# Feed-forward block: the output projection as seven block products of eight, presums started at the input's split, GpSimd left with masks and accumulating DMAs

## The chip, the cores and the metric

One NeuronCore of one Trainium2 chip runs the kernel. The metric is device time in microseconds (us) of one execution; lower is better. Engines are called as the profile calls them: PE (TensorE matmul), PEld (its weight load), DVE (VectorE), ACT (ScalarE), POOL (GpSimd), SP (SyncE, which here only issues DMAs; SPq and POOLq are the queues).

## The reference

One layer of a hybrid encoder over 528 positions (16 learned ones and 512 frames), width 1024, float32:

```python
u  = rmsnorm(h, norm_mix_w)
proj = u @ w_in                         # 1024 x 8208, cut into c, q, k, v, z, a, b, gates
y_conf = silu(layernorm(conv31(c_val * sigmoid(c_gate)))) @ w_conf_out
y_dn = (rmsnorm(gated_delta_rule(silu(conv4(q, k, v)), a, b)) * silu(z)) @ w_dn_out
g_conf, g_dn = split(sigmoid(gate_logits + b_gate))
h = h + (g_conf * y_conf + g_dn * y_dn) @ w_out
u2 = rmsnorm(h, norm_ffn_w)
up = conv3(u2 @ w_up)                   # 1024 x 5632
h = h + (silu(up_gate) * up_val) @ w_down
out = rmsnorm(h, norm_final_w)[:, 16:]
```

## The kernel before

All activations lie transposed, 128 channels on the partitions and the positions along the row, so that a product is a sum over eight channel tiles with the weights as the stationary operand. Every float32 product is made of three passes of a rounded format: the high parts of both factors, high by low, and low by high. `weights` loads one 128x1024 tile of weights into a buffer `wr` (three of them) by a DMA on SP, has ACT cast it to the high part `wh` and DVE subtract to the low part `wl` (two buffers each). `gemm` then issues 8 x 3 x 2 = 48 matmuls of some 260 columns for one output tile of 128 channels.

The stages, with the names of their tiles: keys (`k`) and small decay terms; the convolution branch (`cg`, `cv`, with 30 taps a channel tile on DVE into `ca`); eight heads of the delta rule (`q`, `v`, then short chains `kS`, `wP`, `S`, `o`, whose matmuls are interleaved with products `ga`, `z`); `layer_norm`; the two branch projections (`y`, 8 + 8 tiles, scaled by the gates in `gt`); the output projection (`wo`, 8 tiles); the feed-forward's first product (`up`, 6 tiles, then 19 pairs in `sx` and `sz`); its second product (`dn`); the final norm.

The 19 pairs are made by `seven`: a 256x256 block product in halves, as seven products of 128-row blocks and not eight, each of 12 matmuls of 258 columns (4 pairs of channel tiles x 3 passes), 84 for a pair of output tiles where `gemm` issues 96. Seven products need sums of weight blocks and sums of input blocks. `factors` makes the latter on DVE, one call for two channel tiles, and splits them with ACT and DVE. The former are made ahead by `presums`, all in HBM (tiles `ws`): two plain copies (each 512 KB), then an accumulating DMA of 512 KB and two of 256 KB, each waiting for the one before. In the kernel before all five are on POOL's queue, start after the last mask (`masks[-1]`), and two sets are in flight at a time: the copies of set m wait for the end of set m-2.

POOL also does the masks (`affine_select` in `decays`), 23 memsets of four columns ahead of a convolution row (`ra`, in `out_raw` and `conv4`), 4 memsets `LL` and 32 block copies into `mn` (in `grow`).

A scheduler inside the program (`Plan`) sets the order: it records the operations, gives each a modelled price, and places them by list scheduling with the due times of a table (`BIAS`, `LNP`, `IVP`, `UP`, `WP`). Each engine then runs its list strictly in that order, and so does each DMA queue: an instruction that waits holds up everything behind it on its engine. Every instruction is emitted at line 469, so the profile is read by tile names.

Of the kernel before, what the change touches and what calls it, by code (L numbers as in the profile page):

```python
# [230 lines left out]
class Plan:  # L231
# [66 lines left out]
    def price(self, eng, fn, a, k, out):  # L298
# [10 lines left out]
        if fn == "dma_start":  # L309
            if eng == "POOL":  # L310

                return 1000, int(np.prod(out.shape)) * 4 / 140.0
            return 475, int(np.prod(out.shape)) * 4 / 290.0 * (1 if self.run(k) >= P else 2)
# [158 lines left out]
def record(A, out):  # L472
# [65 lines left out]
    def presums(src, n, hold):  # L538
# [3 lines left out]
        for m in range(n):  # L542
          with plan.at(1):
# [195 lines left out]
    for k in range(KT + 1):  # L739
      with plan.at(UP):  # L740
# [106 lines left out]
    def conv4(acc, t, way=None):  # L847

        c = bt(n="cv")
        if way:  # L850
            a = acc
            if way == "copy":
                a = bt(n="ra")
                G.memset(a[:, :PAD], 0.0)
# [88 lines left out]
    masks, softs = [], []  # L943
# [46 lines left out]
    def grow(h0):  # L990
# [218 lines left out]

    wus = presums(A['wuq'], FT - NPRE, masks[-1])  # L1210
# [55 lines left out]
    mh, ml = [], []  # L1266
# [11 lines left out]
    for f in range(KT):  # L1278
        x = bt(n="xr")
        SY.dma_start(out=x[:, :TW], in_=A['xT'][f][:, T0:T])  # L1280
        acc = p2("wo")
        gemm(acc, weights(A['wo'][f]), mh, ml, MIDR)
# [223 lines left out]
```

## Time and profile before

| | |
|---|---|
| time, median of 3 runs | 1016.2 us (1014.99 to 1018.35) |
| the profiled execution's own time | 1018.73 us |
| its span, first to last instruction | 1016.9 us |
| mean granted TensorE clock | 0.994 |
| busy: PE / DVE / ACT / POOL | 98% / 75% / 52% / 11% of the span |
| DMA moved | 157.39 MB, mean 155 GB/s |

The profile page is of one execution. A busy PE is not PE at its peak: matmuls overlap, and one that waits a short while can still count as busy; how fast products run is read from the distance of matmuls in the chain of work, not from the busy share. Waits name the engine that came last.

### The profile page before, as it was taken

How to read it: one execution, taken by the hardware profiler on the slowest of the kernel's cores; microseconds unless marked ns; L12 is line 12 of the kernel's file. 1: busy time of each engine (PE TensorE's matmuls, PEld its weight loads, DVE VectorE, ACT ScalarE, POOL GpSimd, SP SyncE). 2: the span in 40 equal slices, each digit the busy share in tenths (PEclk: the TensorE clock that was granted, in tenths of full speed). 3: DMA queues.
4: the chain of work that ended last, by engine and by line, in shares of the span. 5: the costliest groups of instructions: out<-in, count | busy, mean ns of one | idle time of the engine just before them, and what ended most of it. 6: DMA issues, size and time to landing. Idle time of an engine off the chain costs nothing.

```text
span 1016.9 us, 20105 instructions
## 1 busy us (share of the span) xinstructions
PE 995.6 (98%) x8202; PEld 949.7 (93%) x8202; DVE 766.4 (75%) x1304; ACT 526.2 (52%) x945; POOL 108.4 (11%) x172
## 2 busy tenths in 40 slices
PE   9999999999999999999999999999999999999996
PEld 6999999999989998989999999999999999988886
DVE  5988959689979998989485455599998988832334
ACT  5688732263644554355373224467786766632222
POOL 0011221523421222120000000000000000000000
PEclk9999999999999999999999999999999999999998
DMA  6144698988688897883313244424555556643332
GB/s 224 63 124 97 174 208 218 254 161 191 178 152 203 217 221 158 206 195 87 123 63 110 98 167 138 133 84 145 176 179 184 189 164 185 206 136 101 99 93 83
DMA packets 67932, 157.39 MB, mean 155 GB/s; under 512 B 15104, under 2 KB 21632, under 8 KB 67840
## 3 DMA queue, kind: packets, MB, share of 16 engines
q1 hardware_dynamic: 51728, 116.26, 36.1%
q0 software_dynamic: 16112, 39.85, 20.4%
q8 instruction: 64, 1.05, 0.4%
q14 instruction: 28, 0.23, 0.1%
HBM read 150.78 MB, written 45.16 MB: 193 GB/s over the span
## 4 chain that ended last, share of the span: by engine, by line
PE 72%; DMA 12%; issue 6%; DVE 5%; ACT 3%; POOL 1%; SPq 0%; DVEq 0%; ACTq 0%; POOLq 0%
PE dn L469 12%; PE sx L469 10%; PE y L469 9%; DMA ws<-in_wuq 7%; PE sz L469 7%; PE wo L469 5%; PE cv L469 5%; PE ga L469 4%; PE cg L469 4%; PE up L469 3%; PE z L469 2%; PE v L469 2%; DMA ws<-ws 2%; DMA eg<-d_e 2%; PE q L469 2%
## 5 line engine op out<-in xcount | busy, mean ns | idle before, releaser
L469 DVE TENSOR_TENSOR wl<-wr,wh 128x1024 fp32r<-128x1024 f32 (+2 forms) x195 | 225.6, 1158 | 156.0 <-PE dn L469 61.6
L469 ACT CAST wh<-wr 128x1024 fp32r<-128x1024 f32 (+2 forms) x195 | 193.8, 996 | 222.0 <-PE dn L469 56.4
L469 DVE SCALAR_TENSOR_TENSOR ca<-c,par,ca 128x516 f32<-128x516 f32 (+10 forms) x240 | 178.4, 750 | 6.3 <-ACT ca L469 2.3
L469 DVE SCALAR_TENSOR_TENSOR uy<-up,par,uy 128x512 f32<-128x512 f32 x88 | 64.2, 746 | 1.8 <-ACT uy L469 1.4
L469 POOL DMA_DIRECT2D ws<-in_wuq x57 | 49.3, 872 | 151.3 <-DMA ws<-in_wuq 77.7
L469 PE MATMUL dn<-fh,wh 128*128 128x512 f32 (+1 forms) x171 | 61.8, 369 | 0.0
L469 PE MATMUL dn<-fl,wh 128*128 128x512 f32 (+1 forms) x171 | 61.8, 369 | 0.0
L469 PE MATMUL sx<-nh,wh 128*128 128x258 f32 x228 | 60.5, 289 | 1.2 <-ACT wh L469 0.9
L469 PE MATMUL sz<-nl,wh 128*128 128x258 f32 x228 | 59.8, 283 | 0.0
L469 PE MATMUL sx<-nl,wh 128*128 128x258 f32 x228 | 59.4, 282 | 0.0
L469 PE MATMUL sz<-nh,wh 128*128 128x258 f32 x228 | 59.4, 283 | 0.0
L469 PE MATMUL ga<-ul,wh 128*128 128x258 f32 (+1 forms) x256 | 59.0, 294 | 0.0
L469 PE MATMUL ga<-uh,wh 128*128 128x258 f32 (+1 forms) x256 | 58.7, 294 | 0.0
L469 DVE SCALAR_TENSOR_TENSOR cv<-ra,par,cv 128x528 f32<-128x528 f32 x69 | 50.8, 758 | 6.2 <-POOL ra L469 5.9
L469 PE MATMUL ga<-uh,wl 128*128 128x258 f32 (+1 forms) x256 | 48.4, 295 | 0.0
L469 POOL DMA_DIRECT2D ws<-ws x38 | 35.8, 951 | 93.6 <-DMA ws<-in_wuq 58.8
L469 PEld LDWEIGHTS sx<-nh,wh 128*128 128x128 f32 x228 | 43.1, 189 | 2.9 <-ACT wh L469 1.4
L469 PE MATMUL sz<-nh,wl 128*128 128x258 f32 x228 | 44.6, 283 | 0.0
L469 PEld LDWEIGHTS sx<-nl,wh 128*128 128x128 f32 x228 | 43.2, 190 | 0.0
L469 PEld LDWEIGHTS sz<-nh,wh 128*128 128x128 f32 x228 | 42.9, 189 | 0.1
L469 PEld LDWEIGHTS sz<-nl,wh 128*128 128x128 f32 x228 | 42.9, 189 | 0.0
L469 PEld LDWEIGHTS ga<-ul,wh 128*128 128x128 f32 x256 | 42.7, 192 | 0.3
(324 smaller groups left out, 2764.7 us busy)
## 6 DMA issues: line engine op xcount, KB each, us to landing
wr<-in_win SPq DMA_DIRECT2D x64, 512.0 KB
ws<-in_wuq POOLq DMA_DIRECT2D x57, 512.0 KB, 7.9
wr<-ws SPq DMA_DIRECT2D x38, 512.0 KB
ws<-ws POOLq DMA_DIRECT2D x38, 256.0 KB, 6.1
wr<-in_wuq SPq DMA_DIRECT2D x19, 512.0 KB
wr<-in_wd SPq DMA_DIRECT2D x17, 512.0 KB
wr<-in_wuq SPq DMA_DIRECT2D x19, 256.0 KB
wr<-in_wdn SPq DMA_DIRECT2D x8, 512.0 KB
```

The source lines that it names most:

```text
L469: getattr(engines[o.eng], o.fn)(*(get(x) for x in o.a), **{n: get(x) for n, x in o.k.items()})
```

## The change

The output projection goes through `seven` as well: 4 pairs of output tiles, 28 block products of 12 matmuls, in place of 8 `gemm` calls of 48. For that, `factors` is called for each two finished tiles of the mix (tiles `mt`, `mq`, `mh`, `ml`, `mhl`), the results are added by DVE straight into the residual (`use`), and `w_out` gets four sets of presums. All presums now start once the input is split (`done`), the 4 sets of `w_out` first. Their two plain copies go from POOL's queue to SP's. The memsets go from POOL to DVE, the copies into `mn` to ACT. The scheduler's price of an accumulating DMA and its table of due times are others, so the order of the whole program differs.

```diff
-                return 1000, int(np.prod(out.shape)) * 4 / 140.0
+                return 1000, int(np.prod(out.shape)) * 4 / 122.0
...
-            G.dma_start(out=r[m][:, 0:2], in_=src[:, m, 0:3:2])
+            SY.dma_start(out=r[m][:, 0:2], in_=src[:, m, 0:3:2])
             plan.after = set(h)
-            G.dma_start(out=r[m][:, 2:4], in_=src[:, m, 0:2])
+            SY.dma_start(out=r[m][:, 2:4], in_=src[:, m, 0:2])
             G.dma_start(out=r[m][:, 1:3], in_=src[:, m, 3:4].broadcast_to([P, 2, HD]), accum_op=ALU.add)
...
-        G.memset(a[:, :PAD], 0.0)
+        V.memset(a[:, :PAD], 0.0)
...
+    softs, done = [], max(j for _, j, w in uh[-1].tl.hist if w)
+    wos = presums(A['wo'], KT // 2, done)
+    wus = presums(A['wuq'], FT - NPRE, done)
...
-            G.memset(l[0:32, :, 32:64], 0.0)
+            V.memset(l[0:32, :, 32:64], 0.0)
...
-                G.tensor_copy(out=Mn[h][r, :, r], in_=D8(h)[r])
+                S.copy(out=Mn[h][r, :, r], in_=D8(h)[r])
...
-
-    wus = presums(A['wuq'], FT - NPRE, masks[-1])
...
-        a, b = split(y[:, :TW], TW, "m")
-        mh.append(a)
-        ml.append(b)
+        ys.append(y)
+        if f % 2:
+            with plan.at("mf"):
+                mb.append(factors(*ys[f - 1:], HW, "m"))
...
-        acc = p2("wo")
-        gemm(acc, weights(A['wo'][f]), mh, ml, MIDR)
-        V.scalar_tensor_tensor(out=halves(x[:, :TW], HW), in0=acc[:, :, MID], scalar=0.5, in1=halves(x[:, :TW], HW),
-                               op0=ALU.mult, op1=ALU.add)
...
+    for m in range(KT // 2):
...
+        x0, x1 = hs[2 * m:]
+        where = {'p1': (x0, 0, 0.5), 'c11b': (x0, 0, 0.5), 'u2': (x0, 1, 0.5), 'c12b': (x0, 1, 0.5),
+                 'u3': (x1, 1, -0.5), 'c22b': (x1, 1, -0.5), 'c21': (x1, 0, -0.5)}
+
+        def use(what, acc):
+            x, b, by = where[what]
+            xb = x[:, b * HW:(b + 1) * HW]
+            V.scalar_tensor_tensor(out=xb, in0=acc, scalar=by, in1=xb, op0=ALU.mult, op1=ALU.add)
+
+        seven(A['wo'], m, wos, mb, HW, use)
```

Of the table only this is shown, since its numbers tell a reader nothing: `SWITCH` 375 to 750, `LNP` -146 to 74, `IVP` 2165 to 665, `UP` 519 to 0, `WP` 214 to 174, and all of `BIAS`. What it does to the order stands below at three places.

**POOL's queue** in the heads stage, before. `ws` are the presums (number of the set, then a serial number), `ra` is the convolution row of a head.

```order
L469 DMA ws_9_3520<-ws_9_3520 128x512
L469 DMA ws_10_3546<-ws_10_3546 128x512
L469 DMA ws_9_3520<-ws_9_3520 128x512
L469 MEMSET ra_10_2071 128x4
L469 DMA ws_10_3546<-ws_10_3546 128x512
L469 DMA ws_11_3988<-in_wuq 128x2x512
L469 DMA ws_12_4037<-in_wuq 128x2x512
L469 DMA ws_11_3988<-in_wuq 128x1024
```

After the change the same queue holds accumulating DMAs alone there; neither memsets nor plain copies (the 128x1024 ones) are left on it:

```order
L469 DMA ws_13_3203<-in_wuq 128x2x512
L469 DMA ws_14_3274<-in_wuq 128x2x512
L469 DMA ws_13_3203<-ws_13_3203 128x512
L469 DMA ws_14_3274<-ws_14_3274 128x512
L469 DMA ws_13_3203<-ws_13_3203 128x512
L469 DMA ws_14_3274<-ws_14_3274 128x512
```

**SP's queue** in the heads stage, after the change: the plain copies stand among the loads of weights (`wr`) and of the heads' decay rows (`eg`), and from the copies of sets 15 and 16 to those of sets 17 and 18 there are two loads of weights. Before, the queue had only the loads there.

```order
L469 DMA wr_40_3634<-in_win 128x1024
L469 DMA ws_15_3660<-in_wuq 128x2x512
L469 DMA ws_16_3754<-in_wuq 128x2x512
L469 DMA ws_15_3660<-in_wuq 128x1024
L469 DMA ws_16_3754<-in_wuq 128x1024
L469 DMA eg_3_3856<-d_e_1_835 128x528
L469 DMA wr_41_3932<-in_win 128x1024
L469 DMA eg_4_3946<-d_e_1_835 128x528
L469 DMA wr_42_4009<-in_win 128x1024
L469 DMA ws_17_4120<-in_wuq 128x2x512
L469 DMA ws_18_4164<-in_wuq 128x2x512
```

**The start of the output projection**, after the change. First DVE, from the scaling of the last branch tile (`y_16`) to the first result of a block product (`sx_1`); `gt_6` and `gt_15` are the last two mix tiles, `ml_10` to `ml_12` the low parts of their factors:

```order
L469 SCALAR_TENSOR_TENSOR gt_6_5102<-gt_6_5102,y_16_7508 128x516
L469 TENSOR_TENSOR gt_6_5102<-gt_6_5102,gt_2_3909 128x516
L469 TENSOR_TENSOR gt_15_6441<-gt_6_5102,gt_15_6441 128x258
L469 SCALAR_TENSOR_TENSOR mt_4_7491<-mt_4_7491,gt_6_5102 128x258
L469 TENSOR_TENSOR ml_10_7625<-gt_6_5102,mh_10_7620 128x2x258
L469 SCALAR_TENSOR_TENSOR mq_4_7630<-mt_4_7491,gt_6_5102 128x258
L469 TENSOR_TENSOR ml_11_7634<-gt_15_6441,mh_11_7623 128x2x258
L469 TENSOR_TENSOR ml_12_7642<-mt_4_7491,mh_12_7628 128x2x258
L469 TENSOR_TENSOR mhl_4_7637<-mq_4_7630,mhl_4_7637 128x258
L469 SCALAR_TENSOR_TENSOR xr_1_7467<-sx_1_7586,xr_1_7467 128x258
```

And PE there: twelve matmuls stand between the last of `y_16` and the first row that needs a factor of the last two tiles (`mh_10`); the rows below begin with the last two of the twelve.

```order
L469 MATMUL sz_1_7595<-mh_4_7344,wh_81_7494 128x258
L469 MATMUL sz_1_7595<-ml_4_7352,wh_81_7494 128x258
L469 MATMUL sz_1_7595<-mh_10_7620,wh_81_7494 128x258
L469 MATMUL sx_1_7586<-mh_11_7623,wh_81_7494 128x258
L469 MATMUL sz_1_7595<-ml_10_7625,wh_81_7494 128x258
L469 MATMUL sz_1_7595<-mh_7_7545,wl_81_7516 128x258
L469 MATMUL sz_1_7595<-mh_1_7268,wl_81_7516 128x258
L469 MATMUL sz_1_7595<-mh_4_7344,wl_81_7516 128x258
L469 MATMUL sz_1_7595<-mh_10_7620,wl_81_7516 128x258
L469 MATMUL sx_1_7586<-ml_11_7634,wh_81_7494 128x258
```

Before, `y_16` needed one addition and one split to follow it on DVE, and the first `wo` product had its other seven channel tiles to go through.

## Rows read from the trace of the kernel before

**Rows 1.** The page: the span, and each engine's busy time.

```profile
span 1016.9 us, 20105 instructions
...
PE 995.6 (98%) x8202; PEld 949.7 (93%) x8202; DVE 766.4 (75%) x1304; ACT 526.2 (52%) x945; POOL 108.4 (11%) x172
```

**Rows 2.** Busy time by stage: from:to length, engines, PEclk, DMA share, GB/s.

```profile
180.00:470.00 290.00, 282.03 (x2664) 271.60 (x2664) 256.14 (x392) 140.72 (x289) 85.06 (x130) 0.99 0.82 189
...
603.00:650.00 47.00, 47.00 (x390) 46.92 (x389) 25.42 (x32) 17.77 (x23) 0.00 (x0) 1.00 0.52 160
650.00:882.00 232.00, 230.64 (x1896) 227.97 (x1895) 210.83 (x325) 163.46 (x262) 0.00 (x0) 1.00 0.53 165
```

**Rows 3.** The chain that ended last: start, length, what, matmul count.

```profile
602.70 46.55 PE wo L469 x384
...
736.83 2.90 PE sx L469 x24
```

**Rows 4.** Timeline, 294 to 297 us: start, length, engine, instruction, [idle before it].

```profile
295.10 0.39 POOL L469 MEMSET ra<- 128x4 f32 x1
...
295.53 0.77 DVE L469 SCALAR_TENSOR_TENSOR cv<-ra,par,cv 128x528 f32<-128x528 f32 x1 [2.83 <-POOL ra L469]
...
296.61 0.49 PE L469 MATMUL wP<-r,mn 128*128 128x128 f32 x2 [2.33 <-DVE r L469]
```

**Rows 5.** Busy time by stage, as rows 2, around that hole.

```profile
280.00:300.00 20.00, 17.64 (x134) 16.47 (x133) 15.51 (x30) 8.91 (x25) 4.91 (x7) 0.95 0.84 138
```

**Rows 6.** Groups of instructions by form: count, busy us, mean ns, idle before.

```profile
L469 POOL COPY mn<-DU 32x128 f32<-32x128 f32 x32 | 18.9, 596 | 2.8 <-DMA DU<-d_x 1.6
...
L469 ACT COPY mn<-gX 32x128 f32<-32x128 f32 x16 | 4.1, 255 | 0.2
```

**Rows 7.** Timeline of DVE, 741 to 746 us, where it works without a pause.

```profile
741.33 0.68 DVE L469 TENSOR_TENSOR uy<-uy,uy 128x512 f32<-128x512 f32 x1
741.93 0.42 DVE L469 TENSOR_TENSOR up<-up,sz 128x258 f32<-128x258 f32 x1
742.26 1.22 DVE L469 TENSOR_TENSOR wl<-wr,wh 128x1024 fp32r<-128x1024 f32 x1
743.40 0.68 DVE L469 TENSOR_TENSOR fl<-uy,fh 128x512 fp32r<-128x512 f32 x1
...
744.66 0.69 DVE L469 TENSOR_TENSOR wl<-wr,wh 128x512 fp32r<-128x512 f32 x1
745.26 0.75 DVE L469 SCALAR_TENSOR_TENSOR uy<-up,par,uy 128x512 f32<-128x512 f32 x1
```

**Rows 8.** Group of DVE by form, 603 to 649 us, as rows 6.

```profile
L469 DVE SCALAR_TENSOR_TENSOR hl<-xr,par,hh 128x516 fp32r<-128x516 f32 x7 | 5.3, 757 | 5.6 <-ACT hh L469 5.6
```

**Rows 9.** Timeline, 603.5 to 606 us, DVE and ACT at the last branch tile.

```profile
603.94 0.68 DVE L469 SCALAR_TENSOR_TENSOR gt<-gt,y 128x516 f32<-128x516 f32 x1
...
604.65 0.70 DVE L469 TENSOR_TENSOR gt<-gt,gt 128x516 f32<-128x516 f32 x1
...
605.38 0.62 ACT L469 CAST mh<-gt 128x516 fp32r<-128x516 f32 x1 [3.50 <-DVE gt L469]
```

**Rows 10.** Timeline of POOL, 299 to 335 us: two sets of presums.

```profile
299.44 0.98 POOL L469 DMA_DIRECT2D ws<-in_wuq  x1
...
311.50 1.19 POOL L469 DMA_DIRECT2D ws<-in_wuq  x1 [6.63 <-DMA ws<-in_wuq]
...
319.15 1.18 POOL L469 DMA_DIRECT2D ws<-in_wuq  x1 [6.35 <-DMA ws<-in_wuq]
...
334.62 0.99 POOL L469 DMA_DIRECT2D ws<-in_wuq  x1
```

**Rows 11.** DMA queues: packets, MB, share of 16 engines' span (q1 SP, q0 POOL).

```profile
q1 hardware_dynamic: 51728, 116.26, 36.1%
q0 software_dynamic: 16112, 39.85, 20.4%
```

**Rows 12.** Instructions on tile wr, 190 to 467 us: ns min/median/max, first to last start.

```profile
L469 SPq DMA_DIRECT2D wr<-in_win x33: 327/328/3490, 190.1 to 466.9; - x33
```

**Rows 13.** Waits of PE over the whole span: us in total, times, longest.

```profile
PE vp L469 <- ACT cv L469: 4.7, 3, 2.4
PE wP L469 <- DVE r L469: 2.3, 1, 2.3
```

More of the change, by code (lines that the diff above doesn't have):

```diff
@@ L162 @@
+LNP = 74
+IVP = 665
+UP = 0
+WP = 174
 WARM = 16
@@ L853, in conv4 @@
                 a = bt(n="ra")
-                G.memset(a[:, :PAD], 0.0)
+                V.memset(a[:, :PAD], 0.0)
                 S.copy(out=halves(a[:, PAD:], 264), in_=acc[:, :, :264])
@@ L941, in grams @@
             SY.dma_start(out=d_m[b, h].rearrange("n j t -> j n t"), in_=mn[32 * b:32 * b + 32, :, 32 * b:32 * b + 32])
-    masks, softs = [], []
+    masks = []
     ivt = {}
@@ L1264, in record @@
     ydn = [call(lambda f: gated(gts[KT + f], A['wdn'][f], oh, ol), "y", f) for f in range(KT)]
-    mh, ml = [], []
+    mb, ys = [], []
     for f in range(KT):
@@ L1269, in record @@
         V.tensor_tensor(out=y[:, :TW], in0=y[:, :TW], in1=ydn[f][:, :TW], op=ALU.add)
-        a, b = split(y[:, :TW], TW, "m")
-        mh.append(a)
-        ml.append(b)
+        ys.append(y)
+        if f % 2:
+            with plan.at("mf"):
+                mb.append(factors(*ys[f - 1:], HW, "m"))
     HS = 2
     hs, hh, hl, sq = [], [], [], []
-    for f in range(KT):
-        x = bt(n="xr")
-        SY.dma_start(out=x[:, :TW], in_=A['xT'][f][:, T0:T])
-        acc = p2("wo")
-        gemm(acc, weights(A['wo'][f]), mh, ml, MIDR)
-        V.scalar_tensor_tensor(out=halves(x[:, :TW], HW), in0=acc[:, :, MID], scalar=0.5, in1=halves(x[:, :TW], HW),
-                               op0=ALU.mult, op1=ALU.add)
-        hs.append(x)
-        hi, lo = bt(F32R, "hh"), bt(F32R, "hl")
-        S.mul(out=hi[:, HS:HS + TW], in_=x[:, :TW], mul=pc('nf', f))
-        V.scalar_tensor_tensor(out=lo[:, HS:HS + TW], in0=x[:, :TW], scalar=pc('nf', f), in1=hi.bitcast(F32)[:, HS:HS + TW],
-                               op0=ALU.mult, op1=ALU.subtract)
-        hh.append(hi)
-        hl.append(lo)
-        s = bt(n="hsq")
-        S.activation(out=s[:, :TW], in_=x[:, :TW], func=AF.Square)
-        if f:
-            V.tensor_tensor(out=s[:, :TW], in0=s[:, :TW], in1=sq[:, :TW], op=ALU.add)
-        sq = s
@@ new lines, in record @@
+    for m in range(KT // 2):
+        for f in (2 * m, 2 * m + 1):
+            x = bt(n="xr")
+            SY.dma_start(out=x[:, :TW], in_=A['xT'][f][:, T0:T])
+            hs.append(x)
+        x0, x1 = hs[2 * m:]
[6 more added lines that the diff above has]
+        seven(A['wo'], m, wos, mb, HW, use)
+        for f in (2 * m, 2 * m + 1):
+            x = hs[f]
+            hi, lo = bt(F32R, "hh"), bt(F32R, "hl")
+            S.mul(out=hi[:, HS:HS + TW], in_=x[:, :TW], mul=pc('nf', f))
+            V.scalar_tensor_tensor(out=lo[:, HS:HS + TW], in0=x[:, :TW], scalar=pc('nf', f), in1=hi.bitcast(F32)[:, HS:HS + TW],
+                                   op0=ALU.mult, op1=ALU.subtract)
+            hh.append(hi)
+            hl.append(lo)
+            s = bt(n="hsq")
+            S.activation(out=s[:, :TW], in_=x[:, :TW], func=AF.Square)
+            if f:
+                V.tensor_tensor(out=s[:, :TW], in0=s[:, :TW], in1=sq[:, :TW], op=ALU.add)
+            sq = s
@@ L1471, in arrays @@
     a['wab'] = np.ascontiguousarray(ab.reshape(KT, P, 32).transpose(1, 0, 2)).reshape(P, KT * 32)
-    a['wco'], a['wdn'], a['wo'] = _pack(w_conf_out[0]), _pack(w_dn_out[0]), _pack(w_out[0])
+    a['wco'], a['wdn'], a['wo'] = _pack(w_conf_out[0]), _pack(w_dn_out[0]), _quarters(w_out[0])
     w = w_up[0].reshape(D, 2, FT, P)
```

8 lines of the change are left out of this document (2 added, 6 removed).

## The prediction

> **What bounds the kernel now.** First the page: PE is busy 995.6 of a span of 1016.9 us, DVE 766.4, POOL 108.4 [rows 1]. So the end is set by how many matmuls PE issues and by how long it waits between them; other engines count only where PE waits for them. The stages come next [rows 2]. Between 603 and 650 us, the output projection, PE is full and DVE has 25.42 of 47 us of work: a stage in which fewer matmuls are a shorter time. From 650 to 882 us, where `seven` is already used, DVE is at 210.83 of 232 us, so that form asks more of DVE. In the heads stage, 180 to 470 us, PE is busy 282.03 of 290 us, so nearly 8 us are plain holes. The waits say what ends them: ACT's `cv` 4.7 us in three, DVE's `r` 2.3 us in one [rows 13]. Last the chain, for the pace: 384 matmuls of `wo` in 46.55 us are 121.2 ns each, and 24 of `sx` in 2.90 us are 120.8 ns [rows 3].
>
> A measurement of this kernel can tell about 0.3%, some 3 us, from no change.
>
> **Fewer matmuls.** 8 x 48 = 384 become 28 x 12 = 336. At the pace of `sx` [rows 3] they take 336 x 0.1208 = 40.6 us in place of 46.55: **-6.0 us**. Nothing hides or delays this, if the stage stays bound by PE.
>
> **DVE in that stage.** Where DVE never pauses, the distance from start to start is its price: 1.14 us for a full `wl`, 0.60 for a half one, 0.33 for adding 258 columns from PSUM, 0.60 for 512 columns [rows 7]; `hl` is at most 0.757 [rows 8]. A pair of output tiles now needs 3 x 1.14 + 0.60 + 7 x 0.33 + 2 x 0.757 + 2 x 0.60 (the squares' sum) = 9.0 us of DVE in 84 x 0.1208 = 10.1 us of PE. That is 89%: PE still leads, but with little room. The nearest measured stage is the one after it, at 91% [rows 2]. Its 19 x 84 + 288 = 1884 matmuls would take 227.6 us at that pace and it lasts 232, a loss of 1.9%. On 40.6 us that is **+0.8 us** (bounds 0 and 4: the latter if each of the 28 additions holds the next product on its bank by a further eighth of a `wl`).
>
> **The start of that stage.** Before, the last branch tile was followed by one addition and a cast; now by factors. I count from the last matmul of `y_16`. DVE starts the scaling 0.15 us later; the addition follows 0.71 us on, the cast 0.73 us after that, and it takes 0.62 [rows 9]. So `mh_10` is ready at 2.2 us and PE may use it at 2.4; the twelve matmuls ahead of it last 1.45 us. Then DVE in the order shown: two ops of 258 columns, the split `ml_10` from 2.35 us, `mq_4`, the split `ml_11` from 3.3 to 3.95 (0.6 each, 0.33 for the small ones). PE reaches row `sx<-ml_11` at 4.2 and ends the first product at 4.7. Its next use of bank `sx_1` waits for the addition at the end of that DVE list, behind `ml_12` and `mhl_4`: 5.3 and some 0.2 for the signal, 5.5 us. Twenty-four matmuls have been issued by then, 2.9 us of work: **+2.6 us** (bounds 0.9, the first wait alone, and 4).
>
> **POOL's memsets.** At 293 us the memset of `ra` stands behind two accumulating DMAs on POOL's queue, as the order shows. It starts at 295.10; DVE has sat idle 2.83 us for it, and PE then 2.33 us for DVE's `r` [rows 4]. On DVE the memset has nothing to wait for: **-2.3 us** (bounds 0, if another late input takes its place, and 2.3). The granted clock of that stretch is 0.95 of the upper level, 2.4 GHz [rows 5], which lies behind the hole; 0.05 x 20 us is 1.0 us of work, **-1.0 us** (bounds 0 and 1.0).
>
> **What I cost at nothing.** The 27 memsets on DVE are dearer than nothing and cheaper than a 258-column op: under 27 x 0.33 = 9 us, in a stage where DVE is idle 34 us [rows 2]. The 32 copies into `mn` cost POOL 596 ns each and should cost ACT about 255, as its own copies of that shape [rows 6]: 8.2 us, where ACT is idle 149 us [rows 2]. If they came in one piece of 16, 4.1 us, the next product's weights, cast one product (48 x 0.121 = 5.8 us) ahead, cover it; without that cover up to 4 us. `factors` for the first three pairs lies beside the branch projections. Loading `wr` first delays the first input tile and moves up the weights; the last input tile lands after the same bytes: 0, bounds -1 and +1.
>
> **The sums and SP's queue.** One pair of sets takes POOL from 299.44 to 334.62 us, 35.2 us; the first accumulation is issued 12.1 us in, the second 7.7 us later, both waiting for copies [rows 10]. Now the copies are on SP's queue, which moved 116.26 MB in 36.1% of 1016.9 us, 317 GB/s, where POOL's moved 39.85 MB in 20.4%, 192 GB/s [rows 11]. Four copies of 0.52 MB are 6.6 us there. With 15.5 us from the second accumulation to the end, a pair takes 22 us at best and 35.2 at worst. I take 26, nearer the former, since both waits in the row end on copies. But each copy now waits on SP for the end of an earlier set, and loads of weights and of `eg` are queued behind it. In the heads stage 33 loads are issued in 276.8 us, one in 8.4 us [rows 12]. By the order, from sets 11 and 12 to sets 21 and 22, five pairs of sets, there are 16 loads (4, 3, 2, 5, 2): 134 us, and three buffers hold a further 25. So SP falls behind only if a pair takes over (134 + 25) / 5 = 31.9 us. At 26 it does not: **0 us** (bounds 0 and +17, at 35.2 us: 176 - 159).
>
> The Trainium skill speaks against that choice (DMA: Bandwidth & Descriptors, section "Issuing engines are not separate DMA queues"): whichever engine starts them, DMAs run on the same 16 engines and interleave, so another queue saves only the time to initiate. By that the pair would stay near 35 us and the whole sum would end at +11 us. The trace agrees in part: the two queues together have only 56.5% of the engines' time, but the accumulations, which are slower, are in POOL's rate.
>
> **The sum.** -6.0 + 0.8 + 2.6 - 2.3 - 1.0 = -5.9 us. All rows are of the execution of 1018.73 us (span 1016.9), so 1012.8 by its own time. That execution is 2.5 us above the median of the runs, 1016.2; from the median it is **1010.3 us**.
>
> **Rivals.**
> *More comes back in the heads stage* (0.18). The other waits, 4.7 us for `cv` [rows 13], and the clock behind them, about 1 us, go as well, since copies no longer queue with accumulations: 1010.3 - 5.7 = 1004.6. For it: they are the largest waits. Against: nothing in the change touches their own operands.
> *DVE eats the saving* (0.19). The start costs 4, the stage 2 and the freed memset is replaced by another late input: 1016.2 - 6.0 + 6 = about 1016. For it: DVE goes from 54% to 89% of the stage [rows 2]. Against: the next stage lives with 91%.
> *SP holds the weights back* (0.13), the slower side: past 31.9 us a pair, PE waits for `wr` in the heads stage; at 35.2 us the price is 17 us: 1010.3 + 17 = 1027. For it: the row of 35.2 [rows 10], and the skill's rule. Against: both queues' rates.
> *New holes from the new order* (0.08). The whole order differs; if it opens holes like those of rows 13 again, 7.0 us and some clock, about 10 us: 1020. For it: PE's waits depend on which product stands beside which chain. Against: no place in the order shows one.
> That the change doesn't do what it says is excluded by the order: 48 matmuls are gone.
>
> **The numbers.** The forecast has 0.42. Faster by over 0.3% (under 1013.2): most of it, 0.38, with the first rival and a little of the second, 0.59. Within 0.3%: 0.19. Slower: 0.22. The forecast's own bounds, from the start's 0.9 to 4 and the memset's 0 to 3.3 us, are 1007 to 1015. With the first rival the range starts at 1001, and it reaches 1021 to take in the last; the case of SP is left out above.
>
> **What would show it.** Right: `wo` gone, 336 matmuls of `sx` and `sz` ahead of `up` in 43 to 45 us, with one wait of 2 to 3 us at their start; no DVE idle time put down to POOL's `ra`; two accumulations after their copies at under 30 us a pair. Wrong: SP's queue waiting on `ws` with ACT's `wh` idle for `wr` in the heads stage; more than 1% of PE's time lost inside the projection; PE's waits for `cv` or `r` larger than 7 us in total.

## The result, and the profile after

The changed kernel takes 1027.07 us (median of 4 runs, 1022.93 to 1030.75) against 1015.6 us for the kernel before beside it: a ratio of 1.0109, 95% interval 1.0064 to 1.0153. It is slower by about 11 us, where 1010.3 us was forecast. The profiled execution took 1026.99 us, 8.3 us more than the profiled one of the kernel before (1018.73, some 3 us above its median); these 8.3 us are what the tables below can place.

| first matmul of, us | before | after | difference | forecast |
|---|---|---|---|---|
| output projection | 602.5 | 607.3 | +4.8 | -3.3 |
| `up` | 649.1 | 658.8 | +9.7 | -5.9 |
| `dn` | 881.6 | 889.4 | +7.8 | -5.9 |
| end of the span | 1016.9 | 1025.2 | +8.3 | -5.9 |

So the projection takes 51.5 us where it took 46.6 and 44.0 were forecast, and 4.8 us more are gone before it begins. The page of the changed kernel, against [rows 1]: PE has 48 matmuls fewer and still waits longer.

```profile
PE 992.8 (97%) x8154; PEld 946.1 (92%) x8154; DVE 786.6 (77%) x1383; ACT 544.1 (53%) x993; POOL 72.4 (7%) x87
```

Busy time by stage of the changed kernel (from:to length, PE, PEld, DVE, ACT, POOL with their counts, granted clock, DMA share, GB/s); the last row is the projection, which answers to the second of [rows 2]:

```profile
40.00:140.00 100.00, 94.01 (x748) 90.15 (x747) 75.94 (x187) 70.96 (x192) 18.83 (x21) 0.98 0.83 193
140.00:300.00 160.00, 152.64 (x1546) 146.45 (x1546) 147.65 (x322) 75.77 (x161) 28.46 (x30) 0.99 0.91 211
300.00:600.00 300.00, 299.37 (x2620) 293.24 (x2621) 225.93 (x343) 139.76 (x252) 24.48 (x26) 1.00 0.59 144
607.30:658.80 51.50, 45.39 (x339) 43.56 (x337) 38.65 (x65) 23.67 (x35) 0.00 (x0) 0.93 0.57 186
```

The first three stretches of the kernel before:

```profile
40.00:140.00 100.00, 98.91 (x802) 95.84 (x801) 83.83 (x199) 74.39 (x198) 13.89 (x16) 1.00 0.52 133
140.00:300.00 160.00, 156.36 (x1593) 151.39 (x1593) 132.01 (x281) 69.54 (x139) 56.02 (x87) 0.99 0.83 194
300.00:600.00 300.00, 295.67 (x2570) 289.15 (x2570) 236.04 (x342) 136.17 (x239) 37.65 (x54) 0.99 0.59 150
```

PE stands idle 6.0 us between 40 and 140 us, 1.1 before; 7.4 us between 140 and 300 us, 3.6 before; 0.6 us between 300 and 600 us, 4.3 before. That is +4.9, +3.7 and -3.7, and the first 40 us differ by 0.1: together the +4.8. The -3.7 is not the hole that the forecast went by. That hole, at 294 us, lies in the second stretch; its wait for `r` is gone there, but more waits than it have come (1.8 and 1.3 us for ACT's `mn`, 1.4 for ACT's `cv`). What went between 300 and 600 us are the waits for `cv`, which the prediction had as a rival. Before (us in total, times, longest):

```profile
PE vp L469 <- ACT cv L469: 4.3, 2, 2.4
```

**The start of the projection.** Timelines of the changed kernel (start, length, engine, instruction, [idle before it]). First PE:

```profile
608.59 0.28 PE L469 MATMUL sz<-ml,wh 128*128 128x258 f32 x1
611.15 0.39 PE L469 MATMUL sz<-mh,wh 128*128 128x258 f32 x1 [2.28 <-ACT mh L469]
...
614.30 0.58 PE L469 MATMUL sx<-mh,wh 128*128 128x258 f32 x1 [0.52 <-DVE xr L469]
614.68 0.42 PE L469 MATMUL sx<-ml,wh 128*128 128x258 f32 x1
614.89 0.42 PE L469 MATMUL sx<-mh,wh 128*128 128x258 f32 x1
```

Then DVE, with the scaling of the last branch tile at 609.03:

```profile
607.55 1.22 DVE L469 TENSOR_TENSOR wl<-wr,wh 128x1024 fp32r<-128x1024 f32 x1
608.69 0.42 DVE L469 TENSOR_TENSOR mhl<-mq,mhl 128x258 fp32r<-128x258 f32 x1
609.03 0.68 DVE L469 SCALAR_TENSOR_TENSOR gt<-gt,y 128x516 f32<-128x516 f32 x1
...
613.82 0.43 DVE L469 SCALAR_TENSOR_TENSOR xr<-sx,xr 128x258 f32<-128x258 f32 x1
```

The first matmul is at 607.3, so all matmuls of the branch tile had been issued by then, but DVE comes to it only at 609.03: a `wl` and the last factor of the pair before stood ahead on DVE. The third block product, due after 24 matmuls (2.9 us), starts at 614.30, 7.0 us in: 4.1 us lost. Then the matmuls come 0.21 us apart where they came 0.121 apart [rows 3]: the granted clock is at the lower of its two levels, 1.2 GHz and not 2.4, until 620 us. By stretches of 5 us:

```profile
607.00:612.00 5.00, 2.58 (x19) 2.13 (x17) 4.93 (x10) 2.17 (x5) 0.00 (x0) 1.00 0.90 318
612.00:617.00 5.00, 4.39 (x23) 3.91 (x23) 3.73 (x7) 1.60 (x3) 0.00 (x0) 0.65 0.07 15
617.00:622.00 5.00, 5.00 (x32) 5.00 (x31) 1.88 (x4) 0.62 (x1) 0.00 (x0) 0.67 0.31 101
622.00:627.00 5.00, 5.00 (x43) 5.00 (x43) 3.82 (x6) 4.39 (x7) 0.00 (x0) 1.00 0.58 195
```

PE's waits in the stage, beside the 2.28 us at 611.15 (us in total, times, longest). `xr` is the addition that frees a bank; 0.5 of the 3.4 us is the wait at 614.30 above.

```profile
PE sx L469 <- DVE xr L469: 3.4, 4, 1.4
PE sz L469 <- DVE xr L469: 0.2, 1, 0.2
```

**The early hole.** The chain of the changed kernel at 52 to 64 us (start, length, what): a load of weights takes 10.35 us to land, and PE waits for what ACT does behind its cast.

```profile
51.97 10.35 DMA wr<-in_win
...
62.34 1.04 ACT wh L469
63.39 0.09 ACT cd L469
...
63.52 0.41 PE gr L469 x2
```

From 50 to 70 us the DMA queues of that execution were these (packets, MB, share of 16 engines): POOL's accumulations (q0) moved 1.42 MB in more of the engines' time than the 2.12 MB of plain transfers (q1) took.

```profile
q0 software_dynamic: 760, 1.42, 48.1%
q1 hardware_dynamic: 672, 2.12, 37.3%
```

Between 60 and 80 us PE is busy 16.92 of 20 us at a clock of 0.91; before, 19.52 at 1.00.

### The profile page after: what moved, and what is told of

The parts are those of the page before. It is cut to its first block, busy times and chain, and to the rows that moved or that the text cites. A ratio compares the mean times of both kernels' runs of the same rounds, so it can differ in the third digit from the quotient of the medians.

```text
span 1025.2 us, 20111 instructions
## 1 busy us (share of the span) xinstructions
PE 992.8 (97%) x8154; PEld 946.1 (92%) x8154; DVE 786.6 (77%) x1383; ACT 544.1 (53%) x993; POOL 72.4 (7%) x87
## 4 chain that ended last, share of the span: by engine, by line
PE 74%; DVE 14%; DMA 6%; ACT 3%; issue 2%; SPq 0%; POOL 0%; DVEq 0%; ACTq 0%; POOLq 0%
PE dn L469 12%; PE sx L469 12%; PE y L469 9%; PE ga L469 8%; PE sz L469 8%; PE v L469 4%; PE z L469 4%; PE q L469 4%; DVE ca L469 3%; DVE wl L469 2%; PE up L469 2%; DMA wr<-in_win 2%; PE k L469 2%; PE o L469 2%; DVE cv L469 1%
## 5 line engine op out<-in xcount | busy, mean ns | idle before, releaser
L469 DVE TENSOR_TENSOR wl<-wr,wh 128x1024 fp32r<-128x1024 f32 (+1 forms) x203 | 232.8, 1149 | 134.9 <-PE dn L469 61.5
L469 ACT CAST wh<-wr 128x1024 fp32r<-128x1024 f32 (+1 forms) x203 | 200.7, 990 | 253.3 <-PE dn L469 56.3
L469 DVE SCALAR_TENSOR_TENSOR ca<-c,par,ca 128x516 f32<-128x516 f32 (+12 forms) x240 | 176.9, 744 | 3.3 <-ACT ca L469 0.5
L469 PE MATMUL sx<-nh,wh 128*128 128x258 f32 x228 | 57.9, 284 | 0.6 <-ACT up L469 0.6
L469 PE MATMUL sz<-nh,wh 128*128 128x258 f32 x228 | 57.3, 282 | 0.0
L469 PE MATMUL sz<-nl,wh 128*128 128x258 f32 x228 | 57.1, 282 | 0.0
L469 POOL DMA_DIRECT2D ws<-ws x46 | 43.6, 948 | 149.2 <-DMA ws<-ws 75.4
L469 PE MATMUL ga<-uh,wl 128*128 128x258 f32 (+1 forms) x256 | 45.0, 288 | 0.0
L469 PEld LDWEIGHTS ga<-uh,wh 128*128 128x128 f32 x256 | 43.3, 189 | 0.5 <-issue 0.4
L469 PE MATMUL dn<-fh,wl 128*128 128x512 f32 (+1 forms) x171 | 39.7, 369 | 0.0
```

Source lines behind the costliest of these rows:

```text
L469: getattr(engines[o.eng], o.fn)(*(get(x) for x in o.a), **{n: get(x) for n, x in o.k.items()})
```

## The experiments

All ratios are to the kernel before on the same chip, with 95% intervals. In those that "keep the order", the scheduler's list is made as in the kernel they start from, and operations get another engine or place only as they are emitted. The changed kernel's ratio, 1.0109, stands beside no other run's. The e runs are from one chip; b_proj7, a_quarters, b_memset_dve and b_i2t from a second; c_i2m, c_i2ma, b_copies_sp and a_presums_as_before from a third; a_no_presums, b_no_presums, b_mem_mn and c_i2mas from a fourth; the last two from a fifth. One program was timed on two of them, b_mem_mn, and gave 0.9955 and 0.9894, so ratios of different chips may be 0.6% apart without any difference in the program.

**e1_copies_pool** (copies back on POOL's queue), **e2_presums_late** (presums 80 us later):

```diff
+        if o.eng == "SP" and name(o) == "ws":          # e1
+            o.eng = "POOL"
...
+    t = [t + 80000 * (name(plan.ops[i]) == "ws") for i, t in zip(seq, plan.t)]   # e2, then sorted by t
```

> The changed kernel with the order of every engine kept as it is; only the 46 plain copies of the presums are issued by POOL's queue again, at the same places. Theory A (SP's queue: weights and mask rows stand behind copies that wait for earlier sets): the early holes of the changed kernel close, PE's idle time from 0 to 600 us falls from 15.8 us to about 11 as before, and the time falls by 4 to 6 us, to some 1022 us. Theory B (the presums run earlier, beside the loads of the first 100 us, whichever queue issues them): the wr load at 52 us still takes about 10 us, the hole at 60 to 65 us stays, time within 2 us of 1027. Theory C (the new order as such): also no change.

> The changed kernel with the order of every engine kept; all DMAs of the presums are moved back in the lists so that the first set starts about 80 us later (near 110 us, where the kernel before started them) and the last ends near 520 us. Theory A and theory B both: the hole of 2.9 us at 60 us and those up to 130 us go, with the lower clock behind them, time 3 to 5 us less than the changed kernel's 1027. Theory C (the new order as such makes those holes): PE's idle time from 40 to 140 us stays at 5.8 us and the time too. If SP's queue is what hurts in the heads stage, the holes should only move to later.

e1: 1.0138 (1.0091 to 1.0185), first matmul of the projection at 617.7 us. Theory A's gain did not come: on POOL the copies ran ahead of the masks and in the first 20 us (PE busy 14.61 of 20 us there, clock 0.76; 14.58 between 120 and 140 us). e2: 1.0108 (1.007 to 1.0146), first matmul at 612.4. The hole at 60 us went, as A and B said, and others opened near the end:

```profile
60.00:80.00 20.00, 19.48 (x159) 18.58 (x158) 13.89 (x37) 12.51 (x31) 2.56 (x4) 1.00 0.50 148
400.00:600.00 200.00, 190.74 (x1640) 187.16 (x1639) 116.33 (x171) 81.12 (x138) 19.96 (x21) 0.97 0.67 160
```

So the early start makes the early hole, but in this order of work the presums cost PE wherever they are put.

**e3_filler** (19 matmuls of unused result put into the wait at the start):

```diff
+    first = [i for i in seq if plan.ops[i].eng == "PE" and name(plan.ops[i]) in ("sx", "sz")][:12]
...
+    return seq[:n] + more + seq[n:]      # more: 19 copies of these, into an own bank
```

> The changed kernel with 19 matmuls more on PE, 2.3 us of work whose result is not used, put after the twelve that stand ahead of the wait for the last factors at the start of the output projection. Theory clock (PE standing still for 2.3 us is what halves its pace from 612 to 622 us): the granted clock stays at 1.00 there, the wait is filled, nothing is pushed back, and the time falls by 2.5 to 3.5 us although work was added. Theory DVE (PE is slow there because it waits for DVE's factors and additions, the clock is a by-product): the start of up stays where it is, time the same or up to 2 us more.

1.0006 (0.9976 to 1.0035). Its timeline at the same place:

```profile
613.24 0.39 PE L498 MATMUL sx<-mh,wh 128*128 128x258 f32 x1 [0.52 <-DVE xr L498]
613.46 0.28 PE L498 MATMUL sx<-ml,wh 128*128 128x258 f32 x1
613.59 0.28 PE L498 MATMUL sx<-mh,wh 128*128 128x258 f32 x1
```

The third product starts 6.95 us after the first, as without the filler (7.02): DVE sets that. But behind it matmuls are 0.12 us apart, the clock is 1.00 throughout, and from there to `up` it takes 42.5 us and not 44.5. Beside the changed kernel's profile, added work saved 2.0 us, all of it clock, where 2.5 to 3.5 were expected.

But e1 and e2 have the same wait of 2.28 us without a filler, and their projection takes 49.4 us as with it, not 51.5. There the low clock fell on the matmuls right behind the wait (0.74 in e2 from 616.9 to 621.9 us), which DVE's factors and additions hold up anyway, and was over when the third product started, at 620.07 us in e2:

```profile
616.28 0.58 PE L491 MATMUL sz<-mh,wh 128*128 128x258 f32 x1 [2.28 <-ACT mh L491]
...
620.29 0.29 PE L491 MATMUL sx<-ml,wh 128*128 128x258 f32 x1
620.42 0.28 PE L491 MATMUL sx<-mh,wh 128*128 128x258 f32 x1
```

So the lower clock behind that wait costs 2 us or nothing, by where it falls; what decides that no run shows. In e4, b_proj7, a_presums_as_before and a_no_presums it reached past the start of the third product, as in the changed kernel (51.3 to 52.2 us for the stage). The ratios differ by much more than 2 us (1.0109 to 1.0006; 1.0087 for e4 on the filler's chip); the profiled executions of the filler and the changed kernel differ by 2.9 us, and what else the other runs gained their profile doesn't show.

**e4_mn_pool** (the copies into `mn` back on POOL):

```diff
+        if o.eng == "ACT" and o.fn == "copy" and name(o) == "mn" and "DU" in read(o):
+            o.eng, o.fn = "POOL", "tensor_copy"
```

> The changed kernel with the order of every engine kept; only the 32 block copies into mn go back from ACT to POOL. Theory ACT (the copies in one piece of 16 hold ACT up between casts of weights): PE's waits for ACT's mn and cv, 4.5 us between 200 and 300 us, fall to under 1.5, the clock of 0.91 at 260 to 280 us goes back to 1.00, time 3 to 5 us less than 1027. Rival (POOL, where a copy takes 596 ns and stands behind accumulating DMAs, is later still): waits for mn of 5 us or more, time equal or up to 5 us more.

1.0087 (1.0046 to 1.0128), not told apart from 1.0109. PE's waits for `mn` only changed their name; of the rival the equal time came true, not the waits of 5 us or more:

```profile
PE gX L494 <- POOL mn L494: 2.1, 1, 2.1
PE gP L494 <- ACT mn L494: 1.6, 1, 1.6
```

**b_proj7** (the projection alone on the kernel before):

```diff
+    wos = presums(A['wo'], KT // 2, masks[-1])
     wus = presums(A['wuq'], FT - NPRE, masks[-1])
...
-        gemm(acc, weights(A['wo'][f]), mh, ml, MIDR)
+        seven(A['wo'], m, wos, mb, HW, use)
```

> The kernel before with the output projection alone changed to seven products of eight; its presums join the others on POOL's queue after the last mask, with the table of before; memsets, copies and queues as before. Theory stage (the stage itself loses: DVE is late with the last factors, the banks wait for DVE's additions, the clock falls behind it): the projection takes 48 to 52 us from its first matmul to the first of up, against 46.6 before and the 43 to 45 of the forecast; everything ahead of it as before; time 2 to 6 us above before. Rival (the stage is only slow in the changed kernel because of its table and queues): 43 to 45 us, time 1 to 4 us below before.

1.0132 (1.0057 to 1.0207). The stage takes 51.9 us, from 605.2 to 657.1, with the same waits as in the changed kernel, so it is no matter of table or queues:

```profile
PE sx L469 <- DVE xr L469: 3.2, 4, 1.4
PE sz L469 <- ACT mh L469: 2.9, 1, 2.9
```

Theory "stage" holds, but not its "ahead of it as before": the projection began 2.7 us later. Nor its time: the medians are 11 us apart, not 2 to 6.

**a_quarters** (on the changed kernel, ACT takes results out of PSUM):

```diff
-        seven(A['wo'], m, wos, mb, HW, use)
+        c = quarters(A['wo'], m, wos, mb, HW, "yo")
+        for x, y in ((x0, c[0]), (x1, c[1])):
+            V.scalar_tensor_tensor(out=x[:, :TW], in0=y[:, :TW], scalar=0.5, in1=x[:, :TW], op0=ALU.mult, op1=ALU.add)
```

> The changed kernel, with the seven results of a pair collected as in the feed-forward's first product: ACT takes four of them out of PSUM, DVE adds three, and DVE adds the two finished tiles to the residual. If PE's waits for xr inside the projection (3.4 us) come from additions queued on DVE while the bank is needed, they fall to under 1 us, and the stage goes from 51.5 to 48 to 49 us; the wait of 2.3 us at the start and the lower clock behind it stay. If DVE's load as such is the limit (it stays the same), the stage stays above 50.5 us. Time 1 to 3 us below the changed kernel's 1027, 0.6 to 1.0% above before.

1.0067 (1.0039 to 1.0096); the stage takes 46.8 us, less than the 48 to 49 expected. Some 2 us of that are the clock, which here too was low only ahead of the third product; beside the 49.4 us of e1, e2 and e3 the gain is 2.6. The waits for `xr` are gone with DVE's load nearly the same (37.1 us in the stage, 38.7 in the changed kernel): what cost was a bank waiting in DVE's queue.

```profile
PE sx L469 <- ACT yo L469: 1.1, 2, 0.6
```

**b_memset_dve** (on the kernel before, memsets alone):

```diff
+        if o.eng == "POOL" and o.fn == "memset" and name(o) in ("ra", "LL"):
+            o.eng = "DVE"
```

> The kernel before with the order of every engine kept; only the 23 memsets of ra and the 4 of LL are issued by DVE at their places. The prediction's term: the 2.3 us in which PE waits at 294 us for DVE's r go, and the clock of 0.95 behind it, 2 to 3.3 us less than before. Rival: another late input takes the place, or the memsets cost DVE elsewhere: within 1 us of before.

0.9943 (0.9918 to 0.9969): 5.8 us less, with 3.1 to 8.3 in the interval. Its profiled execution, one of its slower ones, has the first matmul of the projection 2.6 us earlier and a span 2.7 us shorter. So the term is there; that it is larger than the prediction's 3.3 the runs do not show. PE's wait for `r` is gone and that for `cv` fell from 4.7 us [rows 13]; a later one took part of its place:

```profile
PE o L494 <- DVE cv L494: 3.0, 1, 3.0
PE vp L494 <- ACT cv L494: 2.7, 1, 2.7
```

**b_i2t** (on the kernel before: projection as in a_quarters, two pairs interleaved, presums on POOL after the last mask, a new table):

```diff
+    for g in [[0, 1], [2, 3]]:
...
+        cs, runs = zip(*(quarters(A['wo'], m, wos, mb, HW, "yo") for m in g))
+        for _ in zip_longest(*runs):      # one weight tile of each pair in turn
+            pass
```

> The kernel before with the projection as seven products, its presums on POOL after the last mask, two pairs of output tiles interleaved (the block products of pair 0 and pair 1 alternate by weight tile, so that three products and not one lie between two uses of a bank, and 36 matmuls instead of 12 can run ahead of the last factors), results taken out of PSUM as in the feed-forward, and a table of due times made anew for this order. Theory stage: no wait above 1 us inside the projection, clock 1.00, 42 to 45 us for it, time 2 to 5 us below before and 12 or more below the changed kernel. Rival (89% of DVE is too much in any order): 47 us or more, time equal to before or above.

The stage came out as expected, 43.0 us at a clock of 1.00; PE is idle 2.1 us in it, 1.6 of them for the first weights of `up` and 0.3 for a factor:

```profile
603.70:646.70 43.00, 40.92 (x335) 40.02 (x333) 34.99 (x54) 27.57 (x48) 0.00 (x0) 1.00 0.58 186
```

But the whole is 1.0038 (1.0009 to 1.0067): PE waits 9.4 us for ACT's `cv` in the heads, behind memsets of `ra` queued after four more sets of presums on POOL.

**c_i2m** (b_i2t with b_memset_dve's edit), **c_i2ma** (and the copies into `mn` on ACT):

```diff
+        if o.eng == "POOL" and o.fn == "tensor_copy" and name(o) == "mn":
+            o.eng, o.fn = "ACT", "copy"
```

> The interleaved version (b_i2t) with the order of every engine kept; only the 27 memsets of ra and LL go from POOL to DVE. In b_i2t PE waits 9.4 us in three for ACT's cv, behind 8.3 us in which DVE stands idle for POOL's ra. Theory (the memset of ra, queued behind accumulating DMAs on POOL, is the hole of the heads stage): those waits go, the first matmul of the projection comes 6 to 9 us earlier than 603.7, time 6 to 10 us below b_i2t and 4 to 8 us below before. Rival (another late input takes the place): at most 2 us less than b_i2t.

> As c_i2m, and the 32 block copies into mn by ACT and not by POOL. The prediction's term of 0: same time as c_i2m within 2 us. Rival (in one piece they hold ACT up, as PE's waits for ACT's mn and cv of 4.5 us in the changed kernel suggest): 2 to 5 us more than c_i2m.

c_i2m 0.997 (0.9946 to 0.9995), c_i2ma 0.9913 (0.988 to 0.9946). The first matmul of the projection comes at 599.9 and 594.5 us: 3.8 us earlier than in b_i2t, less than the 6 to 9 expected, and 9.2 with the copies on ACT. Those copies cost nothing here; their move helped, and by more than the 2 us within which the two were expected to agree.

**b_copies_sp** (on the kernel before, the plain copies on SP's queue):

```diff
+        if o.eng == "POOL" and name(o) == "ws" and "accum_op" not in o.k:
+            o.eng = "SP"
```

> The kernel before with the order of every engine kept; only the 38 plain copies of the presums go from POOL's queue to SP's, at their places (none before 110 us). The prediction's term of 0: a pair of sets takes 25 to 30 us, the memsets of ra wait less, time 0 to 3 us below before. Rival (SP holds the weights back): PE waits for wh or wl in the heads stage, new holes of 3 us or more between 110 and 480 us, time 3 to 10 us above before.

1.0043 (1.0025 to 1.0062), slower, as the rival had it but by another way: no weights were missing for long (one wait of ACT for `wr`, 5.5 us), the memsets of `ra` stood longer on POOL behind accumulations that waited for SP's copies. DVE stood idle for them 16.2 us between 110 and 480 us, against 5.9, and a pair takes 37.0 us (130.52 to 463.83 us, nine pairs), not 25 to 30:

```profile
DVE cv L494 <- POOL ra L494: 16.2, 4, 5.4
```

**c_i2mas** (c_i2ma with the copies on SP, the same edit):

> As c_i2ma, and the plain copies of the presums on SP's queue at their places, none before 110 us. With the memsets off POOL nothing else waits there for the accumulations. The prediction's term (SP's queue costs 0): within 3 us of c_i2ma, a pair of sets under 30 us. Rival (SP holds the weights back, which b_copies_sp could not tell from the later memsets): PE waits for wh or wl in the heads stage, 4 us or more above c_i2ma.

1.001 (0.9977 to 1.0043), 1.0% above c_i2ma. That is across two chips; on its own it is 0.55% above b_mem_mn, with which c_i2ma agrees where both were timed on one chip (below), so the cost is some 0.6 to 1.0%. With the memsets off POOL, SP's queue still costs; its profile has the first matmul of the projection at 600.8 us, 6.3 later, and longer waits for `eg`, also loaded by SP (the first row is of c_i2mas, the second of c_i2ma):

```profile
DVE cv L499 <- DMA eg<-d_e: 6.9, 3, 3.4
```

```profile
DVE cv L497 <- DMA eg<-d_e: 2.9, 2, 1.9
```

**a_presums_as_before** (on the changed kernel, e1 and e2 together):

> The changed kernel with the order of PE, DVE and ACT kept, but the presums as before: all five DMAs on POOL's queue, and 80 us later in the lists, so that none runs before 110 us. If the early start and SP's queue make the loss ahead of the projection (4.8 us), its first matmul comes at 600 to 603 us and not at 607.3, time 4 to 7 us below the changed kernel's 1027. If the table of due times and the copies on ACT make it, it stays at 606 or later; moving the presums late alone (e2) gave 612.

1.016 (1.0122 to 1.0199), first matmul at 613.3 us. The expectation failed: the changed kernel's order does not suit the old presums either.

**a_no_presums** and **b_no_presums** (no accumulating DMAs, copies after 480 us in the lists):

```diff
+        plan.ops[seq[n]].eng = "SP"
+        t[n] = 470000 + (t[n] - t[sets[0]]) / 4
+    at = sorted((n for n in t if n not in sets or "accum_op" not in plan.ops[seq[n]].k), key=lambda n: (t[n], n))
```

> The changed kernel with the order of PE, DVE and ACT kept, and without presums ahead of the projection: the accumulating DMAs are left out (so the sums of weight blocks are not made), and the plain copies run after 480 us. If the presums' DMAs make the loss ahead of the projection, wherever they are put, its first matmul comes at 600 us or earlier, against 607.3; if the table's order and the copies on ACT make it, at 605 or later. The projection itself stays at 49 to 52 us.

> The kernel before, with the same left out: no accumulating DMAs, plain copies after 480 us, orders kept. What the presums cost before: the memsets of ra no longer stand behind them, so the 2.3 us and the 4.7 us of PE's waits for r and cv should go, first matmul of the projection at 594 to 598 us against 602.5, time 5 to 9 us below before. If those waits have other causes, 601 or later.

b: 0.9924 (0.99 to 0.9949), first matmul at 597.6. a: 1.0095 (1.0067 to 1.0122), at 608.8, so by its total the presums cost nothing. But the edit disturbed its own measure: the copies ran from 369 us on (398 in b) and held up the end of the heads. Windows of a, then of b up to 400 us:

```profile
0.00:400.00 400.00, 394.38 (x3566) 377.94 (x3567) 360.44 (x745) 229.28 (x503) 6.47 (x18) 0.99 0.35 107
400.00:500.00 100.00, 90.10 (x773) 87.30 (x773) 55.12 (x85) 39.31 (x78) 0.00 (x0) 0.95 0.91 280
```

```profile
0.00:400.00 400.00, 397.86 (x3598) 381.03 (x3598) 344.50 (x692) 222.45 (x475) 25.04 (x77) 1.00 0.32 98
```

A few of a's copies run before 400 us, but its PE loses nothing between 369 and 400 us. Up to 400 us PE is idle 5.6 us in a and 15.2 in the changed kernel (384.81 busy); 2.1 in b and 9.0 before (390.97 busy). The presums cost PE 9.6 us there in the changed kernel and 6.9 before; 3.5 us (5.6 - 2.1) are the order's or the moved operations'.

**b_mem_mn** (the kernel before with the edits of memsets and copies into `mn` alone), then both candidates again on one chip:

> The kernel before with the order of every engine kept; memsets of ra and LL by DVE and the 32 copies into mn by ACT, nothing else. If the gain of c_i2ma (0.9913) comes from these moves alone, the ratio is the same, 0.989 to 0.994. If the interleaved projection gives 3.6 us (46.6 to 43.0 us), it is 0.994 to 0.998.

> c_i2ma once more, beside b_mem_mn on one chip: do the interleaved seven products pay at all? If the stage's 3.5 us (46.5 to 43.0 us) reach the end, the ratio to before is 0.3 to 0.5% below that of b_mem_mn. If the four further presums and the load of DVE give it back in the heads stage, the two agree within 0.2%.

> The kernel before with memsets on DVE and copies into mn on ACT alone, once more, for comparison with c_i2ma on the same chip: 0.994 to 0.997 as measured.

b_mem_mn 0.9955 (0.9926 to 0.9985), above the 0.989 to 0.994 at which the moves alone would be all of c_i2ma's gain; the next pair is the better measure, since it is of one chip. There c_i2ma_r is 0.989 (0.9854 to 0.9925; median 1009.25) and b_mem_mn_r 0.9894 (0.9856 to 0.9932; median 1010.19): both beat the kernel before, and they agree; the moves alone give what c_i2ma gives. b_mem_mn_r lies outside the 0.994 to 0.997 expected for it. The stages of c_i2ma_r (to the projection, it, to `dn`), then of b_mem_mn_r:

```profile
0.00:596.20 596.20, 587.94 (x5277) 567.01 (x5277) 486.13 (x926) 315.29 (x646) 102.11 (x133) 1.00 0.73 179
596.20:639.20 43.00, 40.91 (x335) 40.10 (x333) 35.03 (x54) 27.44 (x48) 0.00 (x0) 1.00 0.58 185
639.20:869.20 230.00, 228.28 (x1881) 226.13 (x1882) 212.42 (x325) 164.11 (x261) 0.00 (x0) 1.00 0.54 169
```

```profile
0.00:593.50 593.50, 588.36 (x5276) 567.93 (x5277) 480.88 (x908) 313.84 (x641) 87.03 (x113) 1.00 0.65 163
593.50:640.10 46.60, 46.60 (x386) 46.52 (x385) 24.98 (x31) 17.76 (x23) 0.00 (x0) 1.00 0.56 166
640.10:873.70 233.60, 231.78 (x1903) 228.83 (x1902) 211.22 (x324) 162.91 (x261) 0.00 (x0) 1.00 0.53 164
```

The seven products, in an order that suits them, take 3.6 us off the stage; 2.7 us of that are lost ahead of it. The stage after gains 3.6 and the end loses 2.5 (137.8 against 135.3 us); with another table in one of the two kernels, this pair does not say why.

## Why the prediction was wrong

The forecast, 1010.3, missed in two places of about 8 us each, the stage (+4.9 against -2.6) and what lies ahead of it (+4.8 against -3.3); after them came 1.4 us less (230.6 and not 232.5 from `up` to `dn`, the end 0.5 longer), which it did not treat. It also took 0.3% for what a measurement can tell; the intervals of the runs here are 0.2 to 0.75% to either side.

- **Fewer matmuls, -6.0: right.** b_i2t took 43.0 us, 2.1 of them waits, where 40.6 were counted.
- **The start, +2.6: too small at one step, "DVE starts the scaling 0.15 us later".** It started 1.75 us after the first matmul of the projection, since a `wl` of 1.22 us and an `mhl` stood ahead on DVE. The rows read from the order began at the scaling, and what DVE had still to do then was not counted. The rest of the chain was sized well: first wait 2.28 us for 0.95, third product at 7.0 us for 5.5, both late by those 1.3 to 1.6 us. Loss 4.1 us.
- **The clock behind that wait: missing.** A wait of a few microseconds was priced at its own length, though the prediction itself priced the clock behind the hole at 294 us. It cost 2.0 us in this execution (beside e3_filler); with the same wait it cost nothing in those of e1 and e2, so the wait alone does not fix it.
- **DVE in the stage, +0.8: wrong step, "the nearest measured stage is the one after it".** There ACT takes four of seven results out of PSUM; here all 28 free their bank by an addition on DVE. A load of 89% was not the limit: a_quarters has nearly the same load, no wait for `xr`, and a stage 2.6 us shorter than in e1 and e2, at a like clock. Measured are 3.1 us of waits for `xr` after the start; the 1.7 us that are left (51.5 - 40.6 - 4.1 - 2.0 - 3.1) stand in no row. The upper bound of 4 named this very mechanism.
- **POOL's memsets, -2.3, and the clock, -1.0: right in kind.** Alone they gave 5.8 us (3.1 to 8.3) by the runs and 2.7 by the profile (b_memset_dve). PE's waits for `cv` [rows 13] hung in part on the same memsets; the rival "more comes back in the heads stage" saw that gain but not that cause. In the changed kernel the waits for `cv` between 300 and 600 us went (-3.7) and the wait for `r` at 294 us too, but other waits took the place of the latter (+3.7 between 140 and 300 us), the bound of 0 that the term had.
- **Memsets on DVE and copies on ACT at 0: no cost shows.** The copies took ACT 8.2 us, as worked out, the longest piece 22 of them. PE waited 3.1 us for `mn`, but putting them back gave nothing (e4), and without the rest of the change moving them cost nothing (b_mem_mn) or gained (c_i2ma).
- **SP's queue at 0: wrong, and so was the pair, "I take 26".** From the first accumulation of the first pair of `w_up`'s sets to that of the tenth, POOL's timeline of the changed kernel takes 293.3 us, 32.6 us a pair, past the break-even of 31.9:

```profile
133.33 1.19 POOL L469 DMA_DIRECT2D ws<-in_wuq  x1 [6.58 <-DMA wr<-in_win]
...
426.60 1.18 POOL L469 DMA_DIRECT2D ws<-in_wuq  x1 [6.25 <-issue]
```

  c_i2ma and c_i2mas differ in the queue of the copies alone, and both take 35.8 us a pair (125.15 to 483.41 and 129.94 to 488.21 us, ten pairs each). The Trainium skill (DMA: Bandwidth & Descriptors, section "Issuing engines are not separate DMA queues") says that starting DMAs on several engines saves only the time to initiate them; these two traces agree. The other queue costs all the same: 0.4% on the kernel before (b_copies_sp), where memsets stood longer behind accumulations that waited for SP's copies, and some 0.6 to 1.0% on c_i2ma, where rows `eg` came later. In the changed kernel itself this cost was not measured apart: e1, which undoes the move, also let the copies run earlier. And weights did not run short, as the rival had it: between 130 and 480 us the changed kernel's list has no wait of ACT for `wr`, and PE waits 0.8 us for a `wl`. The rival had the total, 1027, by a mechanism that does not show; that was luck.
- **The presums' start at the input's split was not priced at all.** Its place is 33 to 115 us, where the prediction looked at no row. There a load of weights took 10.35 us, PE lost 6.0 us between 40 and 140 us against 1.1 before, and the clock fell to 0.91 for 20 us. With the start 80 us later (e2) it lost 2.3 us there, so most of the 4.9 us are the early start's.

Of the signs named, "one wait of 2 to 3 us at the start" and "no DVE idle time put down to POOL's `ra`" came true, and yet the kernel is slower; "43 to 45 us", "under 30 us a pair" and "more than 1% of PE's time lost inside the projection" told it. What stays open is why the changed kernel's order loses 3.5 us more ahead of 400 us even without presums, what decides where the low clock behind a wait falls, and why e3_filler's runs gained more than its profile.

## What to carry to other kernels

When a stage gets fewer matmuls, ask which engine frees each bank and what stands in that engine's queue at that moment, and read the order from well before the first dependent row; a busy share below 90% said nothing on either here. Transfers that nobody waits for are not free: price them in the stretch where they start, against the loads that are due there, and ask of every small instruction behind them on the same queue whether it can go elsewhere: that move alone gave 0.5 to 1% here, and the change of algorithm on top of it nothing that can be told (0.989 against 0.9894). And before a small difference is put down to an edit, have both versions timed on one chip.

## What was unexpected in the hardware

One and the same wait of 2.28 us cost different amounts. In the changed kernel the matmuls of the third product and on came 0.21 us apart, at a clock of 0.65 and 0.67 between 612 and 622 us; with nineteen useless matmuls in the wait they came 0.12 us apart at 1.00; and in e1 and e2, without them, the low clock fell on matmuls that had to wait anyway, and those behind also came 0.12 us apart.

Accumulating DMAs moved 1.42 MB in 48.1% of the engines' time, between 50 and 70 us, where plain ones moved 2.12 MB in 37.3%: twice the time per byte. Their packets were smaller, too (1.9 KB against 3.2 KB), and how much of the difference is that, no run shows.

And the same five DMAs cost a different amount by the queue that issues two of them, with all bytes, orders of other engines and places kept: 0.4% on the kernel before (b_copies_sp, 1.0025 to 1.0062), for what waits behind them.
